# Moving a run-time test (and a branch that is never taken) from the middle of a weight-streaming loop into its last block

## The chip, the cores and the metric

One core of one Trainium2 chip. The metric is the device time of one execution in microseconds, lower is better; three executions of the kernel before took 1631.27, 1631.54 and 1636.5 us (median 1631.54).

## What is computed

One decoder layer on 512 tokens of width 1024 in float32: two token mixers, then a mixture of 64 experts (each 1024 to 512 to 1024, SwiGLU), each token sent to two of them, and a final RMSNorm. What matters here, cut:

```python
def run_block(args):                      # one expert, its tokens
    xb = x_pad[toks]
    hid = jax.nn.silu(xb @ w1[e]) * (xb @ w3[e])
    return (hid @ w2[e]) * wts[:, None]
...
x = x + hierarchical_moe(h, ...)          # sum of the two experts of each token
return rmsnorm(x, final_norm_w)
```

All 64 experts' w1, w3 and w2 (2 MB each, some 400 MB in all) are read from HBM once.

## The kernel before

Up to about 690 us the mixers and the router run. Then `moe` runs 16 blocks (`block`), each of four experts. An expert has room for CAP = 32 tokens, so the four fill the 128 rows of a tile. A block gathers its tokens with one-hot matmuls (`gather`, L1061 to L1065), multiplies by w1 into h1 and by w3 into h3 (L1102 to L1107: for each eighth kt of the width, the four experts g), forms silu(h1) * h3 (L1117 to L1119), transposes it (L1122) into `hid` (L1124, ScalarE), multiplies by w2 into y, and adds y to the residual x2 with one-hot matmuls and additions (L1142, L1143).

The weights come in chunks of 1 MB through a ring of 22 slots (`RING`, tiles `ck0` to `ck20`). Chunk i of a block is w1, w3 or w2 (i // 8), expert i // 2 % 4, half i % 2. Where two slots are one tile (`pair`), both halves of an expert's matrix come as one load of 2 MB. `take` is called ahead of each third of a block, and it first issues (`prefetch`, all on SyncE's queue) the loads of eight more chunks, 22 chunks ahead of use. A load waits until the matmuls that read its slot are done, and for its counter: eight counters count landings in turn, so up to eight loads are in flight. Within a block the order of instructions on each engine is made by a scheduler from the program's order and its dependences.

In the last block w2 comes in four strips of columns (`STRIPS`: 512, 256, 128, 128 wide), and `end` (L1145) goes through y, the additions, the squares for the final norm and the multiplication by its gain (L1183, GpSimd) strip by strip; `finish` scales and writes the output (L1198).

An expert that draws more than 32 tokens is overfull. `more_rounds` (L1031), called behind block 7 (of 0 to 15), turns the largest count of tokens into a number of rounds (L1036 to L1038), loads it into a register of every engine (L1039) and branches (L1040). If it is over 1, `overflow` runs all blocks again for the tokens left over, with weights loaded by ScalarE's queue into the working tile `t1`. With these inputs the branch is not taken. Both sides have to leave the counters of finished work at the same values, so on the side that does nothing each engine waits for its own counter's last value and raises it by what the skipped code would have added; SyncE does so for the eight counters of landed loads, one after the other. Instructions can't be scheduled across the test. The lines that speak of it:

```python
            if b == NB // 2 - 1:
                self.more_rounds(wk, mps, mp)
        nr = nc.values_load(ri[0:1, 0:1], min_val=0, max_val=S // CAP)
        with tc.If(nr > 1):
            self.overflow(wk, mps, mp, nr, self.pos, self.e32, self.wts)
```

Of the kernel before, what the change touches and what calls it, by code (L numbers as in the profile page):

```python
# [32 lines left out]
NB = NE // 4  # L33
# [4 lines left out]
def shape_constants():  # L38

    i = np.arange(128)  # L40
    cols = [
        np.eye(128),
        np.ones((128, 128)),
        np.broadcast_to(i[None, :], (128, 128)),
        np.where(i[None, :] <= i[:, None], 0.0, -1.0e30),
        np.broadcast_to((10000.0 ** (-np.arange(32) / 32.0))[None, :], (128, 32)),
        (i[:, None] < i[None, :]).astype(np.float64),
    ]
    cf = np.concatenate(cols, axis=1).astype(np.float32)

    key, masks = i[:, None], []
    j = np.arange(64)
    masks.append((key % 2 == 0) & (key // 2 == j[None, :]))
    for m in (2, 8):
        sub = np.arange(128 // m)
        for dist in (1, 2, 3):
            for_q = np.repeat(sub[sub % 4 >= dist], m)
            masks.append(key // m == for_q[None, :] - dist)
    cm = np.concatenate(masks, axis=1).astype(np.int32)
    return np.ascontiguousarray(cf), np.ascontiguousarray(cm)  # L60


class Trunk:
    def __init__(self, ctx, tc, a, out):
        self.ctx, self.tc, self.nc, self.a, self.out = ctx, tc, tc.nc, a, out
# [737 lines left out]
    def ring_open(self):  # L803
# [3 lines left out]
        self.queue, self.pairs = [], {}  # L807
        self.order = [(b, i) for b in range(NB) for i in range(24)]

    def moe_open(self):  # L810
        tc, nc, a = self.tc, self.nc, self.a
        xp = self.ctx.enter_context(tc.tile_pool(name="x2", bufs=1, side="right", reuse_waits="tile"))
        self.x2 = xp.tile([128, T, D], F32, name="x2")
        self.wk = self.ctx.enter_context(tc.tile_pool(name="mw", bufs=1, side="right", reuse_waits="tile"))
        self.ring_pool("x", "right")

    def prefetch(self, n, eng):
        goal = min(self.nchunk + n, len(self.order))
        while self.nchunk < goal:
            b, i = self.order[self.nchunk]  # L820
            t = self.ring(self.nchunk)
            part = t
            if b < NB - 1 or i < 16:
                pair = self.paired(self.nchunk) and self.nchunk % 2 == 0
                if pair:
                    t = self.pair(self.nchunk)
                    self.queue.append(t[:, 0:4])
                    self.nchunk += 1
                    part = t[:, 4:8]
                eng.dma_start(out=t.rearrange("p a b -> p (a b)"), in_=self.chunk_src(b * 4, i, 1 + pair))  # L830
            elif (i - 16) in self.STRIPS:


                c0, w = self.STRIPS[i - 16]
                n = 512 // w if c0 + w < D else 1

                more = 4 // n - 1
                ts = [t] + [self.ring(self.nchunk + (j if c0 + w < D else j + 3)) for j in range(1, more + 1)]
                w2 = self.a["expert_w2"][0][b * 4:b * 4 + 4, :, c0:c0 + w].rearrange("e (p r) f -> r p e f", r=4)
                at = lambda ft, ts=ts, n=n, w=w: ts[ft // n][:, :, ft % n * w:ft % n * w + w]  # L840
                for ft in range(4):
                    eng.dma_start(out=at(ft), in_=w2[ft])
                part = lambda g, ft, at=at: at(ft)[:, g]
            else:
                part = None
            if part is not None:
                self.queue.append(part)
            self.nchunk += 1
# [24 lines left out]
    def rows(self, name, e):  # L873
        return self.a[name][0][bass.ds(e, 1)].rearrange("e (p r) f -> p (e r f)", p=128)
# [138 lines left out]
    def moe(self):  # L1013
        tc, nc, a = self.tc, self.nc, self.a
        ctx = self.ctx
        x2 = self.x2
        slb, wts, pos, e32, cnt = self.slb, self.wts, self.pos, self.e32, self.cnt
        mp = self.keep
        for name in ("y0", "y2", "wa", "wb"):
            self.ring_pool(name)  # L1020
        with tc.manual_schedule(engines={mybir.EngineType.SP}):
            self.prefetch(len(self.RING) - self.nchunk, nc.sync)
        wk = self.wk
        mps = ctx.enter_context(tc.tile_pool(name="mops", bufs=1, space=PSUM, reuse_waits="tile"))
        for b in range(NB):
            ready, self.ready = self.ready, None
            self.block(wk, mps, lambda t, j: slb[:, t, j, b:b + 1], wts, self.take, ready, b == NB - 1)
            if b == NB // 2 - 1:
                self.more_rounds(wk, mps, mp)

    def more_rounds(self, wk, mps, mp):  # L1031
        tc, nc, cnt = self.tc, self.nc, self.cnt

        rf = mp.tile([128, 1], F32, name="rf")
        ri = mp.tile([128, 1], I32, name="ri")
        nc.vector.tensor_scalar(out=rf, in0=cnt, scalar1=1.0 / CAP, scalar2=(CAP - 1.0) / CAP - 0.5 + 0.5 / CAP,  # L1036
                                op0=OP.mult, op1=OP.add)
        nc.vector.tensor_copy(out=ri, in_=rf)  # L1038
        nr = nc.values_load(ri[0:1, 0:1], min_val=0, max_val=S // CAP)  # L1039
        with tc.If(nr > 1):  # L1040
            self.overflow(wk, mps, mp, nr, self.pos, self.e32, self.wts)

    def take(self, i):

        if callable(self.queue[0]):
            self.prefetch(1, self.nc.sync)
            return self.queue.pop(0)
        self.prefetch(8, self.nc.sync)
        ts = [self.queue.pop(0).rearrange("p a b -> p (a b)") for _ in range(8)]
        return lambda g, c0, n: ts[2 * g + c0 // 2048][:, c0 % 2048:c0 % 2048 + n]  # L1050

    def gather(self, wk, mps, slot, upto=range(T), state=None):
# [43 lines left out]
    def block(self, wk, mps, slot, wts, chunk, ready=None, last=False):  # L1096

        nc, ident, iota = self.nc, self.ident, self.iota
        xT = ready or self.gather(wk, mps, slot)
        h1 = mps.tile([128, FF], F32, name="h1")  # L1100
        h3 = mps.tile([128, FF], F32, name="h3")
        for i, hp in enumerate((h1, h3)):  # L1102
            c = chunk(i * 8)
            for kt in range(KT):
                for g in range(4):
                    self.mm(hp[32 * g:32 * g + 32], xT[:, kt, 32 * g:32 * g + 32], c(g, kt * 512, 512),
                            kt == 0, kt == KT - 1)  # L1107
        if ready:
            with self.tc.issue_after(self.picked.ins):
                self.route_close(wk, mps)  # L1110
        owT = self.spread(wk, mps, slot, wts)
        if last:
            self.finish_open(wk, mps)

        sg = wk.tile([128, 4, 128], F32, name="t1")
        rows = lambda h: h.rearrange("p (j r) -> p r j", r=4)
        nc.scalar.activation(sg, rows(h1), AF.Sigmoid)  # L1117
        nc.vector.tensor_mul(out=sg, in0=rows(h1), in1=sg)  # L1118
        nc.vector.tensor_mul(out=sg, in0=rows(h3), in1=sg)  # L1119
        ps = mps.tile([128, 4, 128], F32, name="ga", bufs=2)  # L1120
        for i in range(4):
            nc.tensor.transpose(ps[:, i], sg[:, i], ident)  # L1122
        hid = wk.tile([128, 4, 128], F32, name="hid")
        nc.scalar.copy(out=hid, in_=ps)  # L1124
        y = [mps.tile([128, 512], F32, name=f"y{i}") for i in range(2)]
        ysb = wk.tile([128, D], F32, name="xT")
        if last:
            with self.tc.manual_schedule(engines={mybir.EngineType.PE}):
                self.end(wk, mps, chunk, hid, owT, y, ysb)
            return  # L1130
        c = chunk(16)
        for half in range(2):
            for ft in range(4):
                for g in range(4):
                    self.mm(y[half][32 * g:32 * g + 32], hid[:, ft, 32 * g:32 * g + 32],
                            c(g, ft * 1024 + half * 512, 512), ft == 0, ft == 3)
        for half in range(2):
            hs = slice(half * 512, (half + 1) * 512)
            nc.scalar.copy(out=ysb[:, hs], in_=y[half])  # L1139
            for t in range(T):  # L1140
                ps = mps.tile([128, 512], F32, name="cb", bufs=2)
                self.mm(ps, owT[:, t], ysb[:, hs], True, True)  # L1142
                nc.vector.tensor_add(out=self.x2[:, t, hs], in0=ps, in1=self.x2[:, t, hs])  # L1143
# [124 lines left out]
```

## Time and profile before

| | us |
|---|---|
| median of three executions | 1631.54 |
| the profiled execution | 1630.87 |
| its span | 1629.1 |
| TensorE busy in the span | 1374.0 (84%) |
| VectorE busy | 595.9 (37%) |
| ScalarE busy | 342.2 (21%) |
| GpSimd busy | 268.0 (16%) |
| read from HBM | 452.87 MB, 279 GB/s over the span |

The span is what the profiler records; the profiled execution lies 1.8 us above it. PE is TensorE's matmuls, PEld its weight loads, DVE VectorE, ACT ScalarE, POOL GpSimd, SP SyncE; a q behind a name is the engine's sequencer. Times in rows count from the start of the span. An idle time in brackets is followed by what ended it. A matmul in float32 shows as two records.

### The profile page before, as it was taken

The page shows a single profiled execution, that of the slowest core. Times are in us where ns is not written, and L with a number is a line of the kernel's source. Part 1 is how long each engine was busy: PE and PEld are TensorE (multiplying, and loading weights), DVE is VectorE, ACT ScalarE, POOL GpSimd, SP SyncE. Part 2 cuts the span into 40 slices and gives each one's busy share as a digit, 9 for nine tenths or more (in the row PEclk, how much of TensorE's full clock was granted, in tenths as well). Part 3 has the DMA queues.
Part 4 walks back from the last instruction along what each step waited for, and adds up shares of the span by engine and source line. Part 5 has one row for each costly group of instructions (what it writes and reads, how often), then busy time and mean ns, then how long its engine had stood idle before and what let it go on. Part 6 is the DMA issues. An engine that isn't in the chain of part 4 may idle for free. (4 is left out here: it accounts for less than half of the span.)

```text
span 1629.1 us, 20358 instructions
## 1 busy us (share of the span) xinstructions
PE 1374.0 (84%) x8282; PEld 844.3 (52%) x8282; DVE 595.9 (37%) x1444; ACT 342.2 (21%) x754; POOL 268.0 (16%) x294
## 2 busy tenths in 40 slices
PE   6899999999999999988888689776298787688776
PEld 5888787878778889833233224221233133133222
DVE  8657786686853333620211112011021120211123
ACT  5455533223332223410100000000000010000012
POOL 5321233323000000012011011010013011011012
PEclk9999999999999999998998899889599898898898
DMA  5111222222163339599999999999689999999997
GB/s 183 57 46 35 71 78 65 65 65 65 39 194 91 104 92 357 207 384 430 429 429 429 429 428 428 430 429 427 281 338 428 430 429 430 428 429 429 429 425 242
DMA packets 123761, 456.36 MB, mean 280 GB/s; under 512 B 11743, under 2 KB 93325, under 8 KB 97421
## 3 DMA queue, kind: packets, MB, share of 16 engines
q1 hardware_dynamic: 120844, 454.52, 69.4%
q8 instruction: 67, 1.10, 0.3%
q10 hardware_dynamic: 2816, 0.47, 0.2%
q14 instruction: 34, 0.27, 0.0%
HBM read 452.87 MB, written 2.10 MB: 279 GB/s over the span
## 5 line engine op out<-in xcount | busy, mean ns | idle before, releaser
L68 PE MATMUL h<-ck,xT 128*32 128x512 f32 x2048 | 301.3, 656 | 115.4 <-DMA ck<-in_expert_w 102.9
L68 PEld LDWEIGHTS h<-ck,xT 128*32 128x32 f32 x2048 | 72.1, 119 | 330.6 <-issue 163.6
L1084 POOL TENSOR_SCALAR t<-cst,slb,wts 128x128 f32<-128x128 f32 x64 | 50.4, 791 | 988.6 <-PE ga L1065 733.7
L1143 DVE TENSOR_TENSOR x<-cb,x 128x512 f32<-128x512 f32 x120 | 82.9, 691 | 279.7 <-PE cb L68 279.7
L68 PE MATMUL y<-ck,hid 128*32 128x512 f32 (+2 forms) x1088 | 166.9, 583 | 14.4 <-ACT hid L1124 10.1
L1065 PE MATMUL ga<-t,wo 128*128 128x128 f32 x1024 | 124.2, 280 | 43.1 <-DVE t L1062 43.1
L1065 PEld LDWEIGHTS ga<-t,wo 128*128 128x128 f32 x1024 | 118.6, 194 | 65.4 <-issue 63.8
L77 POOL TENSOR_TENSOR wlo<-wraw,whi 128x1024 fp32r<-128x1024 f32 (+3 forms) x52 | 97.5, 1877 | 211.8 <-ACT whi L76 186.1
L68 PE MATMUL z<-hTh,whi 128*128 128x512 f32 x320 | 127.7, 399 | 5.4 <-ACT vh L618 5.3
L68 PE MATMUL z<-hTh,wlo 128*128 128x512 f32 x320 | 126.7, 396 | 0.0
L68 PE MATMUL z<-hTl,whi 128*128 128x512 f32 x320 | 126.1, 394 | 0.0
L68 PE MATMUL cb<-xT,owT 128*128 128x512 f32 (+2 forms) x256 | 120.9, 603 | 2.4 <-DVE xT L1159 2.2
L76 ACT CAST whi<-wraw 128x1024 fp32r<-128x1024 f32 (+3 forms) x84 | 77.5, 922 | 171.6 <-PE z L68 90.3
L68 PEld LDWEIGHTS y<-ck,hid 128*32 128x32 f32 x1088 | 43.9, 111 | 108.1 <-issue 81.1
L1119 DVE TENSOR_TENSOR t<-h,t 128x512 f32<-128x512 f32 x16 | 11.1, 691 | 236.9 <-PE h L68 236.8
L68 PEld LDWEIGHTS cb<-xT,owT 128*128 128x128 f32 x256 | 40.3, 188 | 83.5 <-DVE x L1143 46.9
L68 PEld LDWEIGHTS z<-hTh,whi 128*128 128x128 f32 x320 | 60.7, 190 | 18.2 <-ACT vh L618 5.9
L1118 DVE TENSOR_TENSOR t<-h,t 128x512 f32<-128x512 f32 x16 | 11.1, 691 | 161.2 <-ACT t L1117 161.2
L1139 ACT COPY xT<-y 128x512 f32<-128x512 f32 x30 | 17.6, 585 | 245.5 <-PE y L68 245.5
L68 PEld LDWEIGHTS z<-hTh,wlo 128*128 128x128 f32 x320 | 60.4, 189 | 12.5
L68 PEld LDWEIGHTS z<-hTl,whi 128*128 128x128 f32 x320 | 60.6, 189 | 11.7
L1124 ACT COPY hid<-ga 128x512 f32<-128x512 f32 x16 | 9.4, 585 | 272.0 <-PE ga L1122 272.0
(352 smaller groups left out, 2183.1 us busy)
## 6 DMA issues: line engine op xcount, KB each, us to landing
ck<-in_expert_w SPq DMA_DIRECT2D x171, 2048.0 KB, 34.1
ck<-in_expert_w SPq DMA_DIRECT2D x38, 1024.0 KB, 34.0
wraw<-in_w_in SPq DMA_DIRECT2D x48, 512.0 KB, 3.8
wraw<-in_w_branch_mla SPq DMA_DIRECT2D x8, 512.0 KB, 3.6
wraw<-in_w_branch_hgrn SPq DMA_DIRECT2D x8, 512.0 KB
wo<-in_w_out SPq DMA_DIRECT2D x8, 512.0 KB
xt<-in_x SPq DMA_DIRECT2D x4, 512.0 KB, 7.0
wraw<-in_mla_w_ukv SPq DMA_DIRECT2D x16, 128.0 KB, 2.3
```

Of the source, the lines that this page charges most:

```text
L68: self.nc.tensor.matmul(ps, lhsT=l, rhs=r, start=start, stop=stop)
L76: self.nc.scalar.copy(out=hi, in_=src)
L77: (eng or self.nc.vector).tensor_sub(out=lo, in0=src, in1=hi)
L1065: nc.tensor.matmul(ps[kt // 4][:, kt % 4], lhsT=self.h2[t][:, kt], rhs=oh[:, t], start=(t == 0 and kt % 4 == 0), stop=(t == T - 1), skip_g ...
L1084: nc.gpsimd.tensor_scalar(out=ow[:, t], in0=iota, scalar1=slot(t, 0), scalar2=wts[:, t, 0:1], op0=OP.is_equal, op1=OP.mult)
L1118: nc.vector.tensor_mul(out=sg, in0=rows(h1), in1=sg)
L1119: nc.vector.tensor_mul(out=sg, in0=rows(h3), in1=sg)
L1124: nc.scalar.copy(out=hid, in_=ps)
L1139: nc.scalar.copy(out=ysb[:, hs], in_=y[half])
L1143: nc.vector.tensor_add(out=self.x2[:, t, hs], in0=ps, in1=self.x2[:, t, hs])
```

## The change

`more_rounds` is called in the last block, behind `hid` and ahead of the strips of w2. The overflow path gets working memory of its own, cut by the new class `Slots` out of two ring slots that are free by then, instead of the pool that the blocks use. In the last block w3's chunks are reordered, all first halves of the four experts ahead of all second halves, and loaded one by one (1 MB) rather than in pairs; `take` puts them back in the order of use.

```diff
+class Slots:
+    def __init__(self, slots):
+        self.flat, self.at, self.end = slots.rearrange("p a b -> p (a b)"), {}, 0
+    def tile(self, shape, dtype, name):
+        n = math.prod(shape[1:])
+        if name not in self.at:
+            self.at[name], self.end = self.end, self.end + n
+        t = self.flat[:, self.at[name]:self.at[name] + n]
+        return t if len(shape) == 2 else t.rearrange("p (a b) -> p a b", a=shape[1])
...
     def ring_open(self):
...
+        self.order[-16:-8] = [(NB - 1, 8 + 2 * g + half) for half in range(2) for g in range(4)]
...
     def prefetch(self, n, eng):
...
-                pair = self.paired(self.nchunk) and self.nchunk % 2 == 0
+                pair = self.paired(self.nchunk) and self.nchunk % 2 == 0 and (b < NB - 1 or i < 8)
...
     def moe(self):
...
-            if b == NB // 2 - 1:
-                self.more_rounds(wk, mps, mp)
-    def more_rounds(self, wk, mps, mp):
-        tc, nc, cnt = self.tc, self.nc, self.cnt
+    def more_rounds(self, mps):
+        tc, nc, cnt, mp = self.tc, self.nc, self.cnt, self.keep
...
         with tc.If(nr > 1):
-            self.overflow(wk, mps, mp, nr, self.pos, self.e32, self.wts)
+            self.overflow(Slots(self.pair(len(self.order) + 6)), mps, mp, nr, self.pos, self.e32, self.wts)
     def take(self, i):
...
         ts = [self.queue.pop(0).rearrange("p a b -> p (a b)") for _ in range(8)]
+        if not self.queue or callable(self.queue[0]):
+            ts = [ts[half * 4 + g] for g in range(4) for half in range(2)]
...
     def block(self, wk, mps, slot, wts, chunk, ready=None, last=False):
...
         nc.scalar.copy(out=hid, in_=ps)
+        if last:
+            self.more_rounds(mps)
```

How it moves instructions. In the rows below names such as DMAHW3_49 are the eight counters of landed loads, PE_49, DVE_49, Activation_49 and Pool_49 the engines' counters of finished work; the rows of the code of the overflow path are left out at the dots. Lines of the changed kernel are its own numbers: L1054 and L1055 are the load of the count and the branch, L846 and L858 the loads of chunks and of strips, L82 a matmul.

SyncE in the kernel before, around the test behind block 7 (`ck` is a slot):

```order
L830 DMA ck_8314<-in_expert_w 128x4096 [waits DMAHW0_49,PE_49]
L830 DMA ck_8316<-in_expert_w 128x4096 [waits DMAHW1_49,PE_49]
L1039 TENSOR_LOAD ri [waits DVE_49]
L1040 COMPARE_AND_BRANCH
...
L1040 UNCONDITIONAL_BRANCH [waits DMAHW0_49,DMAHW1_49,DMAHW2_49,DMAHW3_49,DMAHW4_49,DMAHW5_49,DMAHW6_49,DMAHW7_49]
L1039 ISA x2
L830 DMA ck_8890<-in_expert_w 128x4096 [waits DMAHW2_49,PE_49]
L830 DMA ck_8892<-in_expert_w 128x4096 [waits DMAHW3_49,PE_49]
```

SyncE in the changed kernel, around the test in the last block:

```order
L858 DMA ck_10127<-in_expert_w 128x4x128 [waits DMAHW4_49,PE_49]
L858 DMA ck_10127<-in_expert_w 128x4x128 [waits DMAHW5_49]
L1054 TENSOR_LOAD ri [waits DVE_49]
L1055 COMPARE_AND_BRANCH
...
L1055 UNCONDITIONAL_BRANCH [waits DMAHW0_49,DMAHW1_49,DMAHW2_49,DMAHW3_49,DMAHW4_49,DMAHW5_49,DMAHW6_49,DMAHW7_49]
L1054 ISA x2
L1217 DMA out<-ck_10220 128x512 [waits DMAHW6_49,DVE_49]
L1217 DMA out<-ck_10220 128x512 [waits DMAHW7_49,Activation_49]
```

The test with its wait for all eight counters stood between loads of weights; it now stands behind the last strip's loads and ahead of the writes of the output.

VectorE in the kernel before: the additions of block 7, the test, and the first instructions behind it, which make the one-hot tile `t` of block 8:

```order
L1143 TENSOR_TENSOR x_5647<-cb,x_5647 128x512 [waits PE_49] x8
L1039 TENSOR_LOAD ri [waits DVE_49]
L1040 COMPARE_AND_BRANCH
...
L1040 UNCONDITIONAL_BRANCH [waits DVE_49]
L1061 TENSOR_SCALAR t_8836<-cst,slb 128x128 [waits DMAHW3_49,DMAHW2_49,DMAHW4_49,DMAHW1_49,DMAHW5_49,DMAHW0_49,DMAHW6_49,DVE_49,DMAHW7_49,PE_49,Pool_49]
L1061 TENSOR_SCALAR t_8836<-cst,slb 128x128
```

VectorE's first instruction behind the test named all eight counters of loads. In the changed kernel this pair of instructions has no test ahead of it.

TensorE in the changed kernel, in the last block: the end of h3 (`h_10120`; `ck_9914`, `ck_9917` hold the first halves of the four experts, `ck_9920`, `ck_9993` the second halves), the transposes of `hid` (L1139), the test, and strip 0 (`y_10602`):

```order
L82 MATMUL h_10120<-ck_9917,xT 32x512 x2
L82 MATMUL h_10120<-ck_9920,xT 32x512 [waits DMAHW2_49]
L82 MATMUL h_10120<-ck_9920,xT 32x512 [waits DMAHW3_49]
L82 MATMUL h_10120<-ck_9993,xT 32x512 [waits DMAHW4_49]
L82 MATMUL h_10120<-ck_9993,xT 32x512 [waits DMAHW5_49]
...
L1139 MATMUL ga<-cst,t_10237 128x128 x3
L1054 TENSOR_LOAD ri [waits DVE_49]
L1055 COMPARE_AND_BRANCH
...
L1055 UNCONDITIONAL_BRANCH [waits PE_49]
L82 MATMUL y_10602<-ck_9996,hid 32x512 [waits DMAHW6_49,PE_49,Activation_49]
L82 MATMUL y_10602<-ck_9996,hid 32x512 x3
```

Before, the four waits of h3 stood at its first four matmuls (one for each pair); now four stand there, for the first halves, and four behind half of the matmuls, and the test stands between the transposes and strip 0.

## Rows read from the trace of the kernel before

**Rows 1.** The page's 40 slices of the span (40.7 us each): mean busy share of the DMA engines in tenths, and what they moved.
```profile
DMA  5111222222163339599999999999689999999997
GB/s 183 57 46 35 71 78 65 65 65 65 39 194 91 104 92 357 207 384 430 429 429 429 429 428 428 430 429 427 281 338 428 430 429 430 428 429 429 429 425 242
```

**Rows 2.** Stretches of the span: length, busy us of PE, PEld, DVE, ACT, POOL (instructions), granted TensorE clock, DMA share, GB/s.
```profile
1000.00:1100.00 100.00, 76.73 (x436) 26.70 (x429) 17.29 (x35) 7.79 (x17) 13.68 (x21) 0.88 1.01 429
...
1160.00:1170.00 10.00, 0.00 (x0) 0.00 (x0) 0.00 (x0) 0.00 (x0) 0.00 (x0) 0.50 0.71 301
1170.00:1180.00 10.00, 8.08 (x58) 8.11 (x59) 1.92 (x8) 0.00 (x0) 0.00 (x0) 0.73 0.01 2
1180.00:1188.00 8.00, 8.00 (x77) 2.98 (x79) 1.31 (x4) 1.36 (x4) 6.67 (x10) 1.00 0.00 0
1188.00:1190.00 2.00, 2.00 (x24) 0.62 (x20) 0.00 (x0) 0.00 (x0) 1.34 (x3) 1.00 0.60 123
1190.00:1200.00 10.00, 6.70 (x60) 2.24 (x56) 2.68 (x8) 1.67 (x3) 0.00 (x0) 0.96 0.99 418
...
1300.00:1500.00 200.00, 163.00 (x1000) 64.81 (x993) 32.48 (x75) 13.74 (x29) 29.57 (x44) 0.91 1.01 429
```

**Rows 3.** Who waited for whom over the whole span: us in total, times, the longest.
```profile
SPq L1040 <- SPq L1040: 33.4, 2, 28.5
...
DVE t L1061 <- SPq L1040: 40.4, 1, 40.4
```

**Rows 4.** The instructions of the lines of the test (L1040 the branch and the raising of counters, L1039 the load of the count), engine by engine: durations in ns (least, median, most), first and last start in us.
```profile
L1040 SPq EVENT_SEMAPHORE  x8: 17/17/17, 1165.5 to 1170.8; - x8
...
L1040 ACTq EVENT_SEMAPHORE  x1: 17/17/17, 1128.3 to 1128.3; - x1
L1040 PEldq COMPARE_BRANCH  x1: 6283/6283/6283, 1129.4 to 1129.4; - x1
L1040 DVEq COMPARE_BRANCH  x1: 72/72/72, 1130.6 to 1130.6; - x1
...
L1040 PEldq EVENT_SEMAPHORE  x1: 51/51/51, 1135.7 to 1135.7; - x1
...
L1039 ACTq TENSOR_LOAD <-ri x1: 467/467/467, 1122.3 to 1122.3; - x1
L1039 PEldq TENSOR_LOAD <-ri x1: 492/492/492, 1128.8 to 1128.8; - x1
```

**Rows 5.** VectorE's and TensorE's timelines around the test: start, us, engine, line, instructions merged, idle time before and what ended it.
```profile
1171.03 0.48 DVE L1061 TENSOR_SCALAR t<-cst,slb 128x128 f32<-128x128 f32 x2 [40.37 <-SPq L1040]
...
1171.92 9.01 PE L1065 MATMUL ga<-t,wo 128*128 128x128 f32 x64 [41.99 <-DVE t L1062]
1180.86 9.65 PE L68 MATMUL h<-ck,xT 128*32 128x512 f32 x88
```

**Rows 6.** ScalarE's timeline, the writing of `hid` in blocks 3, 7, 11 and 15.
```profile
870.80 0.58 ACT L1124 COPY hid<-ga 128x512 f32<-128x512 f32 x1 [20.92 <-PE ga L1122]
...
1106.43 0.59 ACT L1124 COPY hid<-ga 128x512 f32<-128x512 f32 x1 [20.95 <-PE ga L1122]
...
1363.29 0.58 ACT L1124 COPY hid<-ga 128x512 f32<-128x512 f32 x1 [20.92 <-PE ga L1122]
...
1598.88 0.59 ACT L1124 COPY hid<-ga 128x512 f32<-128x512 f32 x1 [16.61 <-PE ga L1122]
```

**Rows 7.** TensorE's timeline in the last block (h1 and h3, the transposes, strips 0 and 1), with VectorE's product that stands between.
```profile
1574.40 7.07 PE L68 MATMUL h<-ck,xT 128*32 128x512 f32 x62
1584.01 1.05 PE L68 MATMUL h<-ck,xT 128*32 128x512 f32 x2 [2.54 <-DMA ck<-in_expert_w]
...
1588.87 8.46 PE L68 MATMUL h<-ck,xT 128*32 128x512 f32 x58 [3.82 <-DMA ck<-in_expert_w]
1597.38 0.69 DVE L1119 TENSOR_TENSOR t<-h,t 128x512 f32<-128x512 f32 x1 [14.38 <-PE h L68]
1598.21 0.63 PE L1122 MATMUL ga<-cst,t 128*128 128x128 f32 x4 [0.88 <-DVE t L1119]
1599.52 3.64 PE L68 MATMUL y<-ck,hid 128*32 128x512 f32 x32 [0.68 <-ACT hid L1124]
...
1607.60 1.45 PEld L68 LDWEIGHTS y<-ck,hid 128*32 128x32 f32 x32 [0.76 <-DMA ck<-in_expert_w]
```

**Rows 8.** Short stretches (columns as in rows 2): behind TensorE's last matmul ahead of the test, at a rise of the clock in block 7, and in the last block.
```profile
1134.00:1135.00 1.00, 0.00 (x0) 0.00 (x0) 0.00 (x0) 0.00 (x0) 0.00 (x0) 0.68 1.07 426
...
1096.00:1099.00 3.00, 3.00 (x16) 0.59 (x12) 0.00 (x0) 0.00 (x0) 0.00 (x0) 0.50 1.01 431
1100.00:1101.00 1.00, 1.00 (x16) 0.28 (x12) 0.00 (x0) 0.00 (x0) 0.00 (x0) 0.88 0.88 377
...
1585.00:1586.00 1.00, 0.06 (x1) 0.00 (x0) 0.00 (x0) 0.00 (x0) 0.00 (x0) 0.50 0.91 377
1591.00:1592.00 1.00, 1.00 (x8) 0.20 (x4) 0.00 (x0) 0.00 (x0) 0.00 (x0) 0.62 1.06 408
1611.00:1613.00 2.00, 2.00 (x38) 1.41 (x36) 1.38 (x2) 0.93 (x4) 1.42 (x2) 1.00 0.13 37
```

**Rows 9.** GpSimd's first multiplication by the gain (timeline), and SyncE's writes of the output (instructions of L1198; columns as in rows 4).
```profile
1606.82 4.69 POOL L1183 TENSOR_TENSOR ck<-x,ck 128x1024 f32<-128x1024 f32 x2 [46.66 <-DMA ck<-in_expert_w]
...
L1198 SPq DMA_DIRECT2D out<-ck x8: 364/454/601, 1620.9 to 1624.8; - x8
```

## The prediction

> **What bounds the kernel now.** I read the slices of the span first: from the second third on the DMA engines are full at 427 to 430 GB/s, except for two slices near 70% of the span that show 6 and 8 tenths and 281 and 338 GB/s [rows 1]. So the expert stage runs at the speed of its weights, and what one change there is worth is the DMA time that it gives back or loses. Next the stages: 1.01 of the engines and 429 GB/s on both sides of the gap, and between 1160 and 1200 us hardly anything moves for 20 us [rows 2]. Third, who waits: SyncE waits 33.4 us at L1040, the branch of the test, and VectorE 40.4 us for SyncE there [rows 3]. Fourth, the steps of that test on each engine [rows 4], and what stood still behind it [rows 5]. Last, the final block, where the test now stands [rows 7 to 9].
>
> What these say together: SyncE comes to the test only after it has issued every load that the 22 slots allow. On the side of the branch where nothing overflows it must see each of the eight load counters reach its last value before it raises it. So all loads in flight drain; the second long wait ends at the last of its eight steps, at 1170.8 [rows 4]. Meanwhile it issues nothing. VectorE is the one behind it: its first L1061 after the test waits for the raised counters, because the overflow path loads into the same working tile (the order of before shows all eight counters on that row). TensorE then gathers from 1171.9 and frees the first slot only when it has run through the first w1 pairs, from 1180.9 on [rows 5]; loads flow again from about 1188.9 [rows 2].
>
> **What the gap is worth.** In 1160 to 1200 us 10 x 301 + 10 x 2 + 2 x 123 + 10 x 418 = 7456 (us times GB/s) moved, where 40 x 429 = 17160 would have; 9704 / 429 = 22.6 us. By busy share: (40 x 1.01 - 7.1 - 0.1 - 1.2 - 9.9) / 1.01 = 21.9 us. By the blocks: hid is written at 870.80 and 1106.43 (four blocks, 235.6 us) and at 1363.29 and 1598.88 (four blocks, 235.6 us); between, four blocks took 256.9, so 21.3 us more [rows 6]. I take **22.0**, between the ends 21.3 and 22.6. The block time of 58.9 us is the same ahead of the gap and behind it, so the full slots that TensorE had after the drain were worth nothing later, and nothing but this gap is lost with the test. In the changed kernel no row on SyncE stands between the loads of block 7 and those of block 8; the eight blocks behind follow at 58.9 us.
>
> **The halves.** In the last block TensorE finishes h1 at about 1581 and has then only waits: the third w3 pair lands at 1584.0, the fourth at 1588.87, 4.9 us apart, and 58 of its 64 records (two a matmul) are still to run, to 1597.33 [rows 7]. With all first halves ahead of all second halves, in the same bytes, the last 1 MB still lands at 1588.87, but kt 0 to 3 of all four experts has then been done: four half loads of 2.4 us earlier their last piece landed, at 1579. Left are 13 of 32 matmuls, 26 records. Full speed is 7.07 us / 62 = 0.114 us a record, half speed twice that. The clock is at half from about 1585 and back after some 2.9 us of work [rows 8]: 12.7 records in 2.9 us, 13.3 in 1.5, and 0.4 of tail, 4.8 us where 8.46 were. So hid is ready **3.7 us earlier**. Ends: 8.46 - (26 x 0.114 + 0.4) = 5.1 if the clock never fell, since TensorE is now busier before; 0 if the halves don't arrive as I think. I take 3.7, as the same gap shows the lower clock in the nearest row. The eight smaller loads keep 8 MB behind the eight counters, 19.5 us at 429 GB/s, so they starve nothing.
>
> **The test at its new place.** Behind hid each engine loads the count and branches. TensorE took 0.49 us for the load and 6.28 us for the branch, and resumed at 1135.75, 6.95 us after 1128.8; ScalarE 6.0 us (1122.3 to 1128.3); VectorE 0.07 us for the branch [rows 4]. This was hidden before (all waited for SyncE anyway) and is now on the path, since strip 0 stands behind it on TensorE. The transposes come at 1598.21 - 3.7 = 1594.5; the load is read behind the last of them, 1594.65; TensorE goes on at 1601.6. ScalarE, whose skip raises the counter that strip 0 waits for, is through at 1598.88 - 3.7 + 6.0 = 1601.2. Strip 0 started at 1599.52, so **+2.1**. TensorE idles some 6 us before it. After the test in the middle its clock fell 4.7 us after its last matmul (0.68 of the slice 1134 to 1135) [rows 5, 8], so strip 0 starts at half: about 2.9 us at half speed cost 1.45, I take **+1.5** (0 if the branch is short, 2.3 if the rise takes over 4 us of work, as in block 7, where half speed lasted from before 1096 to 1100). Behind strip 0 no slack is left: TensorE goes from its combines straight into strip 1 at 1607.6, whose loads had landed 0.8 us or less before (the weight load names the DMA) [rows 7]. So the end moves by 2.1 + 1.5 = **+3.6**. Ends: -0.6, where loads of strip 1 and later bind however early strip 0 is; +5.9, with 1.5 us more for a branch whose code arrives through queues now full of the strips' small rows, and 2.3 for the clock.
>
> [...]
>
> Off the path: GpSimd's skip is done while w3 lands. Its first multiply with the gain (L1202 after) now names all eight load counters; the built program asks for at most 672 of each there, which loads ahead of the strips already give, so it follows strip 0 as before (4.69 us from 1606.82) [rows 9]. SyncE reaches the test after the last strip load and leaves it with the last landing: data stop before 1613 [rows 8], 3.7 us from the last bytes to the last step as in the middle (1167.1 to 1170.8), 1615 at the latest; its next work, the output, was due at 1620.9 [rows 9], so some 9 us cover it. VectorE has 8 us before its copy of strip 0. The other memory of the overflow path costs nothing while it isn't taken.
>
> **Sum.** Profiled time 1630.87 (span 1629.1): 1630.87 - 22.0 + 3.6 = **1612.5**. The median of the runs lies 0.7 above that execution; I leave the sum as it is. Its own ends: 1630.87 - 22.6 - 0.6 = 1607.7 and 1630.87 - 21.3 + 5.9 = 1615.5.
>
> **Rivals.** (1) The branch is short on TensorE and ScalarE, since the place in the code differs: 1630.87 - 22.0 - 0.6 = 1608.3. For it: VectorE's 0.07. Against: the skipped code is as long as before. 0.08. (2) The halves do nothing (the change doesn't do what its words say): 1630.87 - 22.0 + 3.6 + 3.7 = 1616.2. Against: the order puts the matmuls of the first halves ahead. 0.08. (3) The drain moves with the test: strip 0 waits for SyncE, 1615 instead of 1599.5, +15.4 and 1.5 for the clock, 1625.8, which is no measurable change at 0.3%. For it: that is what before did. Against: TensorE's strip row waits for its own load, TensorE and ScalarE, not for all counters. 0.06. (4) **Slower**: as (3), but SyncE's leaving comes first and TensorE's branch of 6.95 us after it: +15.4 + 6.95 + 1.5 = 23.9, 1632.7; it decides above 22.0, and with an output that waits for SyncE's own missed code (6 us) 1638.7. Against: in the middle TensorE branched at 1129.4, long before SyncE was through. 0.03.
>
> **How the numbers follow.** Forecast 0.75, rivals 0.08, 0.08, 0.06, 0.03. A measurement of this kernel tells about 0.3%, 4.9 us, from no change. Faster: 0.75 + 0.08 + 0.08 + a little of (3), 0.92. Same: the rest of (3) and half of (4), 0.06. Slower: 0.02. The range takes the sum's ends and rivals (1) and (2): 1607.5 to 1616.8.
>
> **What would show it.** Right: no slice under 9 tenths of DMA between 45% and 95% of the span; hid of blocks 7 and 8 58 to 60 us apart where 92.3 were; h3's last matmul 4 to 5 us after the last w3 landing; TensorE idle 6 to 7 us between the transposes and strip 0, at half clock after it; SyncE's eight steps at the end without anyone behind them. Wrong: a first y of strip 0 that names SyncE, a TensorE branch under 1 us or over 9, or blocks 8 to 15 above 59.5 us each.

## The result, and the profile after

The changed kernel takes 1617.65 us, the median of five runs (1613.84 to 1619.28), beside 1635.76 for the kernel before (1631.27 to 1637.33): ratio 0.9891, 95% interval 0.9868 to 0.9914, **faster by 1.1%**. The traced execution took 1613.84 us (span 1612.0). Forecast were 1612.5 and at most 1616.8. The direction agrees with it, and so does the traced execution; the median lies 0.85 us above the range.

The slices of the changed kernel's page (40.3 us each), to set beside [rows 1]:

```profile
DMA  5111222222144338589999999999999999999995
GB/s 185 58 47 35 71 67 67 65 70 62 53 156 119 96 100 307 210 367 430 429 429 429 430 430 428 429 428 429 429 429 429 429 428 429 430 429 428 428 416 195
```

The two low slices are gone. So is the late block 8, though its `hid` follows that of block 7 after 60.6 us and not after the 58 to 60 that the prediction named. ScalarE's timeline, `hid` in blocks 7, 8 and 15, to set beside [rows 6]:

```profile
1106.71 0.58 ACT L1141 COPY hid<-ga 128x512 f32<-128x512 f32 x1 [20.95 <-PE ga L1139]
1167.33 0.58 ACT L1141 COPY hid<-ga 128x512 f32<-128x512 f32 x1 [23.11 <-PE ga L1139]
...
1574.06 0.58 ACT L1141 COPY hid<-ga 128x512 f32<-128x512 f32 x1 [12.75 <-PE ga L1139]
```

TensorE's timeline at the last landing of w3 in blocks 3, 14 and 15, and behind it [rows 7]:

```profile
860.57 9.05 PE L82 MATMUL h<-ck,xT 128*32 128x512 f32 x58 [2.92 <-DMA ck<-in_expert_w]
...
1509.01 9.10 PE L82 MATMUL h<-ck,xT 128*32 128x512 f32 x58 [2.89 <-DMA ck<-in_expert_w]
...
1568.90 3.62 PE L82 MATMUL h<-ck,xT 128*32 128x512 f32 x26 [1.37 <-DMA ck<-in_expert_w]
1573.39 0.63 PE L1139 MATMUL ga<-cst,t 128*128 128x128 f32 x4 [0.88 <-DVE t L1136]
1580.64 5.70 PE L82 MATMUL y<-ck,hid 128*32 128x512 f32 x32 [6.62 <-PEq L1055]
```

The start of a row that waits for the DMA is taken here as the time of the landing, and tells how far the weight stream has come. In the kernel before, the same rows of blocks 3 and 14 were these (block 15's is in [rows 7], at 1588.87):

```profile
859.90 9.43 PE L68 MATMUL h<-ck,xT 128*32 128x512 f32 x58 [2.92 <-DMA ck<-in_expert_w]
...
1530.36 8.71 PE L68 MATMUL h<-ck,xT 128*32 128x512 f32 x58 [2.93 <-DMA ck<-in_expert_w]
```

From block 3 to block 14 it is 670.46 us before and 648.44 now: the gap was worth 22.02. In the last row of the changed kernel (strip 0), 6.62 us of waiting are put down to TensorE's own sequencer at the branch. The instructions of the branch's line, engine by engine (columns as in [rows 4]), and who waited for it:

```profile
L1055 SPq EVENT_SEMAPHORE  x8: 17/17/17, 1589.2 to 1592.4; - x8
...
L1055 DVEq COMPARE_BRANCH  x1: 72/72/72, 1573.2 to 1573.2; - x1
...
L1055 PEldq COMPARE_BRANCH  x1: 6286/6286/6286, 1574.0 to 1574.0; - x1
...
L1055 ACTq EVENT_SEMAPHORE  x1: 17/17/17, 1579.1 to 1579.1; - x1
L1055 PEldq EVENT_SEMAPHORE  x1: 51/51/51, 1580.4 to 1580.4; - x1
...
  PEld y L82: 6.8, 1
  PE y L82: 6.6, 1
```

The branch takes TensorE what it took in the middle (6.29 us here, 6.28 in [rows 4]); nobody waits for SyncE's eight steps now. GpSimd and the output follow strip 0 as before [rows 9]:

```profile
1590.00 4.69 POOL L1202 TENSOR_TENSOR ck<-x,ck 128x1024 f32<-128x1024 f32 x2 [50.79 <-DVE x L1186]
```
```profile
1604.13 4.50 SPq L1217 DMA_DIRECT2D out<-ck  x8
```

TensorE's clock in the last block is the last column but two (columns as in [rows 2]); strip 0 (1580.64 to 1586.34) ran at a mean of 0.63:

```profile
1570.00:1580.00 10.00, 3.15 (x22) 0.90 (x14) 0.69 (x1) 0.58 (x1) 0.00 (x0) 0.90 1.01 351
1580.00:1590.00 10.00, 8.55 (x39) 2.82 (x40) 2.08 (x3) 0.77 (x3) 0.00 (x1) 0.76 0.93 265
```

### The profile page after: what moved, and what is told of

It reads as the page before. It is cut to its first block, busy times and chain, and to the rows that moved or that the text cites. A ratio compares the mean times of both kernels' runs of the same rounds, so it can differ in the third digit from the quotient of the medians.

```text
span 1612.0 us, 20365 instructions
## 1 busy us (share of the span) xinstructions
PE 1388.1 (86%) x8282; PEld 845.7 (52%) x8282; DVE 595.9 (37%) x1444; ACT 342.2 (21%) x754; POOL 268.1 (17%) x294
## 5 line engine op out<-in xcount | busy, mean ns | idle before, releaser
L82 PE MATMUL h<-ck,xT 128*32 128x512 f32 x2048 | 314.3, 667 | 124.8 <-DMA ck<-in_expert_w 110.1
L82 PEld LDWEIGHTS h<-ck,xT 128*32 128x32 f32 x2048 | 75.8, 120 | 349.9 <-issue 162.2
L82 PE MATMUL y<-ck,hid 128*32 128x512 f32 (+2 forms) x1088 | 170.5, 584 | 16.1 <-ACT hid L1141 9.4
L82 PE MATMUL z<-hTh,whi 128*128 128x512 f32 x320 | 127.7, 399 | 5.5 <-ACT vh L632 5.4
L82 PE MATMUL z<-hTh,wlo 128*128 128x512 f32 x320 | 126.5, 395 | 0.0
L82 PE MATMUL z<-hTl,whi 128*128 128x512 f32 x320 | 126.3, 395 | 0.0
L82 PE MATMUL cb<-xT,owT 128*128 128x512 f32 (+2 forms) x256 | 120.9, 603 | 2.4 <-DVE xT L1178 2.2
L82 PEld LDWEIGHTS y<-ck,hid 128*32 128x32 f32 x1088 | 43.6, 111 | 110.3 <-issue 92.6
L82 PEld LDWEIGHTS cb<-xT,owT 128*128 128x128 f32 x256 | 40.3, 188 | 83.5 <-DVE x L1162 46.9
L82 PEld LDWEIGHTS z<-hTh,whi 128*128 128x128 f32 x320 | 60.6, 189 | 18.3 <-ACT vh L632 6.0
L82 PEld LDWEIGHTS z<-hTh,wlo 128*128 128x128 f32 x320 | 60.5, 189 | 12.4
L82 PEld LDWEIGHTS z<-hTl,whi 128*128 128x128 f32 x320 | 60.6, 189 | 11.6
```

Source lines behind the costliest of these rows:

```text
L82: self.nc.tensor.matmul(ps, lhsT=l, rhs=r, start=start, stop=stop)
```

## The experiments

The traced execution came out 1.3 us above the forecast, the median 5.2 above. The question was where these are. For every kernel its trace is cut at three landings of the last w3 chunk (blocks 3, 14, 15; TensorE rows that wait for the DMA) and at the end of the span. The first column is the time of the first landing, the next three are the stretches between the cuts, all in us. Each kernel was timed beside the kernel before, whose median of that round stands in brackets; a ratio in the text is to that one.

| kernel | block 3 lands | to block 14 | to block 15 | to the end | median of runs (kernel before) |
|---|---|---|---|---|---|
| before | 859.90 | 670.46 | 58.51 | 40.23 | 1635.76 |
| before, second trace | 862.77 | 670.04 | 58.52 | 40.27 | 1633.41, one run (1635.81) |
| changed | 860.57 | 648.44 | 59.89 | 43.10 | 1617.65 (1635.76) |
| changed, second trace | 865.30 | 648.43 | 59.97 | 42.80 | 1617.98 (1634.38) |
| test last, w3 in pairs | 862.46 | 648.45 | 59.95 | 50.04 | 1622.59 (1634.38) |
| no test | 864.08 | 651.97 | 60.35 | 37.40 | 1616.08 (1634.38) |
| short path (slipped) | 864.41 | 652.01 | 60.68 | 37.40 | 1616.33 (1634.38) |
| short path, in place | 866.61 | 652.03 | 60.56 | 38.90 | 1617.88 (1633.60) |
| test in the middle, halves | 861.77 | 670.26 | 59.01 | 38.06 | 1631.19 (1633.60) |
| middle, own tiles | 863.11 | 653.51 | 59.25 | 40.73 | 1618.29 (1633.60) |
| middle, own tiles, halves | 862.98 | 653.29 | 59.90 | 37.43 | 1615.28 (1635.81) |
| test after h1 | 864.99 | 648.43 | 97.88 (both) | | 1612.27 (1633.60) |

**The same kernels again.** No edit.

> The changed kernel once more, for a second trace. The theory that the runs of one program differ in a stage ahead of the experts: the last landing of w3 of block 14 lies some us away from 1509.0, and the stretch from that landing to the end of the span (103.0 in the first trace) agrees within 0.5 us. The rival, that they differ in the stage that weight transfers bound: block 3's last w3 lands at 860.57 within 1 us, and the stretch from block 3's to block 14's landing (648.4) differs. Median 1614 to 1619.

> The kernel before once more, for a second trace of it. If the runs of a kernel differ only ahead of the experts, where short stretches of TensorE at half clock fall in other places each time, block 3's last w3 lands some us away from 859.9, and from there on the trace repeats the first: block 14's landing 670.5 us behind it within 0.3, block 15's another 58.5 within 0.2, the end 40.2 behind that within 0.5. If the stretch behind the experts' start differs, those three stretches move.

The changed kernel: 1617.98 us (ratio 0.9899, 0.9882 to 0.9916). Both second traces repeat the first behind block 3's landing within 0.5 us (the 670.46 came back as 670.04, where 0.3 was allowed); they differ ahead of it, by 4.73 and 2.87. So the first theory holds for these two pairs, and the rival falls. That the untraced runs differ in the same stage is likely by this, but not shown. Where the 4.73 arise is seen by comparing the changed kernel's two traces start by start. TensorE in the second one, ahead of the experts:

```profile
177.09 0.63 PE L82 MATMUL z<-hTh,whi 128*128 128x512 f32 x1
177.52 0.63 PE L82 MATMUL z<-hTl,whi 128*128 128x512 f32 x1
```

The same matmuls in the first trace:

```profile
175.75 0.40 PE L82 MATMUL z<-hTh,whi 128*128 128x512 f32 x1
175.98 0.39 PE L82 MATMUL z<-hTl,whi 128*128 128x512 f32 x1
```

And the second trace's stretches there (columns as in [rows 2]):

```profile
177.00:178.00 1.00, 1.00 (x4) 0.71 (x4) 0.77 (x4) 0.92 (x4) 0.00 (x0) 0.50 0.12 33
...
249.00:250.00 1.00, 1.00 (x4) 0.75 (x3) 0.00 (x0) 0.00 (x0) 1.00 (x1) 0.50 0.00 0
```

For some 3 us at each place (176 to 179 and 248 to 251) TensorE's granted clock was 0.50 to 0.52 while it was busy; the first trace has 1.00 at both. What TensorE did before doesn't tell them apart: ahead of these places it had waited 1.76 and 1.80 us for VectorE and ScalarE in the second trace, 1.76 and 1.79 in the first. The start-by-start lag grows by some 1.6 us at each of these two places and stays: here each of them moved what stood behind it. The other 1.5 us come in smaller steps elsewhere (0.6 of them by 99 us), whose cause wasn't followed.

**The halves undone.** The line `self.order[-16:-8] = ...`, the condition on `pair` and the two lines in `take` are taken out of the changed kernel.

> The test stays in the last block, but the last w3 comes in chunks of 2 MB again. Theory: the last w3 lands 1.4 us earlier against block 14's landing (58.5 behind it instead of 59.9), h3 behind the landing takes 8.5 us instead of 3.6, hid is ready 3.5 us later, strip 0 starts 3.5 later, and the time is 3.5 us above the changed kernel (ratio 1.002). Rival: the end is bound by strip 1's landing, and the time stays within 1 us.

1622.59 us (0.9935, 0.9916 to 0.9953): 4.6 above the changed kernel by the medians, and 6.9 to 7.2 longer from the last landing to the end in the traces (50.04 against 43.10 and 42.80). The last w3 lands 59.95 behind block 14's, as with the halves, so my reading that smaller loads land later falls. TensorE:

```profile
1570.86 9.89 PE L82 MATMUL h<-ck,xT 128*32 128x512 f32 x58 [3.35 <-DMA ck<-in_expert_w]
...
1589.10 5.88 PE L82 MATMUL y<-ck,hid 128*32 128x512 f32 x32 [6.85 <-PEq L1054]
```

9.89 where 3.62 stand with the halves: more work is left behind the last landing, and the clock is lower too (58 records at a mean clock of 0.71, 0.17 us each; 26 at 1.00, 0.14 each).

**The halves alone, test in the middle.** The same edits, made in the kernel before.

> The kernel before with the halves alone; the test stays in the middle. It parts two readings of why the changed kernel's last w3 lands 59.9 us behind block 14's and not 58.5. If 1 MB chunks cost it, it lands 59.9 behind here too. If the stop at the test lines the 16 DMA engines up again and they drift apart without it, it lands 58.5 behind here, as in the kernel before. h3 then takes 3.6 to 5 us behind the last landing (8.46 before), and the time is 3.5 to 5 us below the kernel before (the pairs run lay 4.6 above the changed kernel).

1631.19 us beside 1633.6 (0.9986, 0.9976 to 0.9996): 2.4 gained, less than the 3.5 to 5 expected. The 26 records took 6.55 us, at a granted clock of 0.55; `hid` came 1.9 earlier behind the landing. The landing is 59.01 behind block 14's, between the two readings. The table sets the two edits apart: with pairs it is 58.5 behind the stop of 22 us in the middle, 59.25 behind one of 5 us and 59.95 without a stop, so moving the test by itself gives the whole 1.4 us. The halves add 0.5 to 0.65 where there is a stop and nothing where there is none (59.89, 59.97; 60.4 to 60.7 in the three kernels with slower loads, see below). Why the stop matters isn't settled.

**No test.** `self.more_rounds(mps)` is taken out of the changed kernel.

> Leaves out the test for overfull experts and the whole path behind it; the rest is the changed kernel. It tells what the test still costs in its new place. Theory: TensorE starts strip 0 when hid is ready, 5.9 us sooner than in the changed kernel, and at full clock (3.64 us instead of 5.70), and then waits for strip 1, which has landed by some 1587: 3.3 us less than the changed kernel. Rival: the loads of the strips don't bind either, and all 8 us come out.

1616.08 us (0.9890, 0.9874 to 0.9906). From the last landing to the end 37.40 instead of 42.80, so the test still costs **5.4 us** in its new place, more than the 3.3 expected and less than the rival's 8. In three kernels this stretch ends at 37.4 whatever h3 took behind the landing (5.81 us here, 5.46 and 4.09), and in the other two of them the last load of strip 0 ends a wait 10.7 us behind the landing: with the loads as they are, a test that cost nothing would end no earlier. The time fell by 1.9 only, which the intervals don't tell from nothing, since block 3 to block 14 took 651.97 instead of 648.43. All three kernels in which the overflow path was cut have these 3.6 us, and in the slices of the expert stage 425 to 428 GB/s where the changed kernel has 428 to 430; the others have not. The transfers themselves are longer here (between 1200 and 1500 us the mean of a 16 KB packet is 615.8 ns, in the changed kernel 613.4). What makes it isn't settled, and the medians of these three are read with it.

**A short path behind the branch.** First the body was one copy on VectorE (`nc.vector.tensor_copy(out=rf, in_=cnt)` in place of `self.overflow(...)`).

> Leaves out the overflow path's computation (its body is one copy on VectorE); the test and its branch stay. Theory: the 6.3 us of TensorE and the 5.0 us of ScalarE at the branch are the price of a target far away in the program, so here TensorE's branch takes under 1 us, strip 0 starts within 1 us of hid, and the time is 3 us below the changed kernel. Rival: the branch costs its 6 us whatever lies behind it, and the time is that of the changed kernel.

1616.33 us. This missed its aim: the scheduler moved the test behind nearly everything, to 1598.6 on TensorE, where its branch took 0.24 us, so place and length changed together. So a body was made that holds the test in place:

```diff
-            self.overflow(Slots(self.pair(len(self.order) + 6)), mps, mp, nr, self.pos, self.e32, self.wts)
+            t = Slots(self.pair(len(self.order) + 6)).tile([128, 2, 128], F32, name="t1")
+            for i in range(2):
+                y = mps.tile([128, 512], F32, name=f"y{i}")
+                nc.tensor.transpose(y[:, 0:128], self.ident, self.ident)
+                nc.scalar.copy(out=t[:, i], in_=y[:, 0:128])
+            nc.vector.tensor_copy(out=rf, in_=cnt)
```

> Leaves out the overflow path's computation; its body is two transposes, two copies on ScalarE and one on VectorE, which write the banks that strip 0 takes, so that the test stays where it is in the changed kernel (in the first run with a short body it slipped to 1598 on TensorE, where its branch took 0.24 us). Theory: a near target costs under 0.5 us here too, strip 0 starts 1 us behind hid, and the stretch from the last landing of w3 to the end is 37 to 38 us as in the run without the test (37.4) instead of 43. Rival: at this place, under full transfers, the branch takes its 6.3 us wherever the target lies, and the stretch is 43.

The line of the branch, and TensorE behind it:

```profile
L1055 PEldq COMPARE_BRANCH  x1: 228/228/228, 1584.3 to 1584.3; - x1
```
```profile
1585.14 3.11 PE L82 MATMUL y<-ck,hid 128*32 128x512 f32 x24 [0.82 <-ACTq L1055]
1589.83 1.06 PE L82 MATMUL y<-ck,hid 128*32 128x512 f32 x8 [1.58 <-DMA ck<-in_expert_w]
```

Same place, loads still running (the last of strip 0 ends a wait at 1589.83), and 0.23 us instead of 6.29: here the price hangs on what is skipped. What moves beside the branch can be seen too, since the trace lists the transfers that bring instructions, of 8 and 16 KB. In the changed kernel three of them start at 1576.96, 1577.18 and 1577.78, while the branch stands (1574.0 to 1580.3); in the kernel before three start between 1131.56 and 1134.33 (branch 1129.4 to 1135.7); here none starts between 1573.2 and 1600.7. The queues of these transfers on the two pages, first the changed kernel's, then this one's (packets, MB, share):

```profile
q8 instruction: 67, 1.10, 0.3%
q14 instruction: 32, 0.26, 0.0%
```
```profile
q8 instruction: 65, 1.06, 0.3%
q14 instruction: 28, 0.23, 0.0%
```

That TensorE waits for code in the long branch is my reading of this and not shown: the trace doesn't say which engine a transfer serves. Strip 0 starts 5.9 us behind the landing (11.7 in the changed kernel), its last load then binds, and the end is 38.90 behind the landing, not the 37 to 38 expected: the first combines behind strip 0 took 3.50 us here, at a granted clock of 0.56, and 1.98 or 1.99 in the other kernels. The time doesn't show the gain, 1617.88 (0.9902, 0.9886 to 0.9917): the 3.6 us of slower loads stand against it, and in the traced execution (span 1618.1) the latest start of all, 866.61.

**The gap taken apart.** The kernel before, test in the middle; only the tiles into which the overflow path loads move, out of the working tile `t1` that the blocks use (and become a quarter of the size, so the skipped path holds four times as many loads):

```diff
+        self.ov = ctx.enter_context(tc.tile_pool(name="ov", bufs=1, reuse_waits="tile"))
...
-                        t = wk.tile([128, 512], F32, name="t1")
-                        nc.scalar.dma_start(out=t, in_=self.chunk_src(e0, i + 2 * g, 2)[:, c0:c0 + n])
-                        return t
+                        for q in range(0, n, 128):
+                            t = self.ov.tile([128, 128], F32, name="tv")
+                            nc.scalar.dma_start(out=t, in_=self.chunk_src(e0, i + 2 * g, 2)[:, c0 + q:c0 + q + 128])
+                            yield q, t
```

> The kernel before, test in the middle, pairs for w3; only the overflow path's loaded tiles lie in a place of their own, so that VectorE's tile behind the test has no load that it must wait for. Theory of the gap (22 us = some 6 us in which SyncE waits for every load + 16 us in which the slots come free late, because VectorE waits for the counters that SyncE raises): the loads stop at 1167 as before, but start again some 6 us later, and the time is 16 us below the kernel before. Rival: the stop of SyncE alone makes the 22 us, and the time is that of the kernel before.

1618.29 us (0.9905, 0.9892 to 0.9918): 15.3 below the kernel before, test and drain where they were. SyncE's eight steps take 5.3 us as before, but VectorE, which waited 40.4 us for this line [rows 3], now waits 4.9, the longest of all that wait for it:

```profile
L1047 SPq EVENT_SEMAPHORE  x8: 17/17/17, 1168.7 to 1174.0; - x8
...
  DVE t L1068: 4.9, 1
```

The loads are off for some 5 us, not 20, as the last w3 of blocks 3 and 14 shows, 653.51 us apart:

```profile
863.11 8.63 PE L68 MATMUL h<-ck,xT 128*32 128x512 f32 x58 [2.92 <-DMA ck<-in_expert_w]
...
1516.62 9.54 PE L68 MATMUL h<-ck,xT 128*32 128x512 f32 x58 [2.93 <-DMA ck<-in_expert_w]
```

So of the 22 us, 17 were the shared tile (670.46 - 653.51) and 5 SyncE's own wait (653.51 - 648.44). With the halves added:

> The kernel before with both: the overflow path's loaded tiles in a place of their own, and the last w3 in halves; the test stays in the middle. If the two add, block 3's landing to block 14's is 653.5 us as in the run with the tiles alone, the last w3 lands 59.3 to 59.8 behind block 14's, the stretch from there to the end is 38 us as in the run with the halves alone (40.7 with the tiles alone), and the time is 2 to 2.5 us below the run with the tiles alone: about 1616, within 2 us of the changed kernel. If the halves gain as much as in the pair of runs with the test in the last block, it is 4.6 below: 1613.7.

1615.28 us (0.9887, 0.9863 to 0.9911). That is 3.0 below the run with the tiles alone by the medians, but the two intervals overlap; in the traces the stretch behind block 14's landing is 2.65 shorter. As good as the changed kernel, by another way.

**The test where TensorE waits anyway.** In the last block `spread`, `finish_open` and `more_rounds` go between h1 and h3, and TensorE keeps the written order there. To have banks and a tile to spare, the path's h1 and h3 take the banks of y, and its loads have tiles of their own (as above).

```diff
+        with self.tc.manual_schedule(engines={mybir.EngineType.PE}) if last else contextlib.nullcontext():
...
+                if last and i == 0:
+                    owT = self.spread(wk, mps, slot, wts)
+                    self.finish_open(wk, mps)
+                    self.more_rounds(mps)
...
-        if last:
-            self.more_rounds(mps)
```

> The changed kernel with the test on TensorE between h1 and h3 of the last block (some 1560 us), where TensorE waits for weights anyway; h1 and h3 of the overflow path share the banks of y, and its loaded tiles have a place of their own. Theory: the branch's 6.3 us lie beside the loads; h3 ends 5 to 6 us behind the last landing (4.5 in the changed kernel), strip 0 starts 7.5 us behind it (11.7) and at full clock, and the stretch from the last landing of w3 to the end is 38 to 39 us instead of 43: 4 to 5 us less. Rival: the halt lets the clock fall, h3 runs at half clock to 9 us behind the landing, and the time is within 1 us of the changed kernel's.

1612.27 us (0.9868, 0.9852 to 0.9884), the lowest median of all. It lies 5.4 to 5.7 below the changed kernel's two medians; these were timed in other rounds, and by the ratios it is 3.8 to 5.1. TensorE, from block 14's landing on:

```profile
1513.42 8.77 PE L93 MATMUL h<-ck,xT 128*32 128x512 f32 x58 [2.93 <-DMA ck<-in_expert_w]
...
1570.48 9.27 PE L93 MATMUL h<-ck,xT 128*32 128x512 f32 x64 [5.62 <-PEq L1074]
...
1582.00 3.64 PE L93 MATMUL y<-ck,hid 128*32 128x512 f32 x32 [0.73 <-ACT hid L1164]
```

The branch stands from 1564.4 to 1570.4, beside the loads. TensorE idled 5.6 us there, the clock fell (0.51 from 1570.4 to 1575) and h3 took 9.27, as the rival said. Yet TensorE waits only 0.73 us, for `hid`, ahead of strip 0, which runs at full clock (3.64), and the span ends 97.88 us behind block 14's landing, where the changed kernel took 102.99 and 102.77: 4.9 to 5.1 us less. No row shows the last landing of w3 here, since TensorE came to h3 late.

## Why the prediction was right and wrong

- **The base was the step that failed.** "The median of the runs lies 0.7 above that execution; I leave the sum as it is." The sum started from one execution, 1630.87, the fastest of the four that were known; one of these, 1636.5, lay 5.6 above it, and that was treated as nothing. The five runs of the result have their median at 1635.76, 4.9 above that base. The step itself was near: 18.4 us were forecast, 18.1 lie between the two medians (16.4 in the next round, 1634.38 and 1617.98), and from 1635.76 the same sum gives 1617.4, beside the 1617.65 measured.
- What made that execution fast shows in its trace: block 3's last w3 landed at 859.90, earlier than in any of the other eleven, which lie between 860.57 and 866.61. The nine traces without the slower loads have a mean of 862.65, and with it the sum would have been 1612.5 + 2.75 = 1615.3 and the range's upper end 1619.6, above the medians that came (1617.65, 1617.98). That mean could not be known then; the spread of the four times could. It was also bad luck that two of the three runs shown were among the fast ones. From trace to trace, both early (859.90, 860.57), the step was 17.0.
- **The gap**: 22.0 forecast, 22.02 measured, and its cause as told: SyncE's wait for every load in flight, then VectorE behind the raised counters. What I hadn't split is that 17 of it hang on the shared tile alone.
- **When the last w3 lands** was taken as unchanged, for no other reason than "in the same bytes". It came 59.89 behind block 14's instead of 58.51: **1.4 us lost**, which moving the test gives by itself (59.95 with pairs). Why it does stays open.
- **The halves**: `hid` 4.85 us earlier behind the landing (10.01 before, 5.16 now), 3.7 forecast. The clock stayed full here (1.00 over the 26 records, 3.62 us), so the gain came near the bound of 5.1 that I had named; in the run with the test in the middle the clock fell (0.55) and 1.9 was left. By the run that undoes them the halves are worth 4.6 to 7.2.
- **The branch**: 6.29 us where 6.28 was forecast; no run shows the 1.5 us more that the upper end allowed for code through full queues (6.27 and 6.56 in two more traces). Strip 0 starts 11.74 behind the landing, before 10.65: +1.1 where +2.1 was forecast, the difference being the halves. Its lower clock (0.63, before 1.00) cost 5.70 - 3.64 = 2.1, forecast 1.5. What follows strip 0 took 0.3 less than before.
- Summed from trace to trace: -22.0 + 1.4 + 1.1 + 2.1 - 0.3 = -17.7, and +0.7 that the changed kernel's experts began later: -17.0. The terms were sound to 1 us together, in part because the halves' 1.2 more and the landing's 1.4 nearly cancel, which is luck. None of the rivals came. Rival (2) falls with the run without halves, (1) with the row of the branch, (3) and (4) since nobody waited for SyncE. No run shows the 6 us that (4) had for SyncE's code: its branch took 0.05 us at 1589.0, and its steps began at 1589.2. One reading among the rivals was wrong: (3)'s 1625.8 lies 5.1 below the profiled 1630.87, more than the 4.9 that the prediction itself calls measurable.
- The price of the branch, measured both ways: 6.29 us with the path as it is, 0.23 with a short one in the same place. VectorE's took 0.07 for the long one. Three transfers of instructions start inside the long branch (1576.96 to 1577.78 in the changed kernel) and none beside the short one; that a branch which skips more waits longer for them fits the two runs, but no row shows it.

## What to carry to other kernels

A forecast of a few us needs the spread of the stages ahead of the change, not one execution: cut two traces of the same kernel at the same landings, see which stretch repeats, and put the sum on the mean of the one that doesn't. A path that was never run still cost here SyncE's wait for the counters that its skip must raise (5 us) and TensorE's branch over it (6.29 us); look first at who shares a tile with the skipped path (17 us here), then put the test where its engine waits for data anyway (5 us).

## What the runs showed of the hardware

- In one trace of the changed kernel TensorE's granted clock was 0.50 for some 3 us while it was busy, at 177 and at 249 us; in the other it was 1.00 there, behind waits of the same 1.8 us in both. These two places made 3.2 of the 4.73 us between the two traces; over all twelve the landing in block 3 spreads by 6.7 us (5.4 among the nine with the full weight rate).
- The weight stream repeats to 0.02 us over 648 (648.43 to 648.45 in four traces of three programs), yet takes 652.0 in three programs in which the overflow path was cut or left out, with longer packets in the run without the test (615.8 ns, 613.4 in the changed kernel). Why is open.
- The skipped path of full length cost TensorE 6.28 us (before) and 6.29 us (changed) at the branch, in which three transfers of instructions start, and a short one in the same place 0.23 us, without such transfers; VectorE paid 0.07 us for the long one in both.
